# A gated up projection by seven products a pair: every second pair, summed in PSUM

## The chip, the core and the metric

The kernel runs on one core of a Trainium2 chip. The metric is the time of one execution in device microseconds; the smaller the better. Three runs of the kernel before are shown, and one execution of it that was taken by the hardware profiler.

## The reference

One layer of a hybrid encoder trunk in float32: a mixing part (attention and a gated scan, with an output projection), cross attention into 256 memory tokens, and a gated feed-forward part with a convolution over positions. There are 512 positions of width 1024. Only the last part matters here:

```python
def conv_ffn(h, w_up, conv_w, conv_b, w_down):
    n = h.shape[1]
    u = h @ w_up                                  # (512 x 1024) @ (1024 x 5632)
    half = CONV_W // 2
    up = jnp.pad(u, ((0, 0), (half, half), (0, 0)))
    acc = conv_b
    for j in range(CONV_W):                       # CONV_W = 3
        acc = acc + up[:, j:j + n] * conv_w[j]
    gate, val = jnp.split(acc, 2, axis=-1)
    return (jax.nn.silu(gate) * val) @ w_down     # (512 x 2816) @ (2816 x 1024)
```

## The kernel before

**Arithmetic.** Each float32 matrix is split into a rounded high part and a low part (the rest), and each product is made of three matmuls: high by high, high by low, low by high (`mm3`, L296 to L298). The three accumulate in one PSUM bank.

**Weights.** A weight unit is a block of 128 x 1024 float32. SyncE loads it into a raw room (`load_w`, L207); ScalarE casts its high part (L240); the low part is made by DVE (L242), or, for some, by a negation on ScalarE (L247) and an accumulating DMA from DRAM issued by GpSimd (L248). High and low parts lie in four slots, `wh` and `wl`; a unit's cast waits until TensorE is done with the unit that held the slot. Raw rooms are few too: a load waits until the last reader of the room's block is done. Units are asked for up to three ahead, loads up to seven (`issue_ahead`).

**The up projection.** The 5632 columns are 22 pairs of 128 gate columns and 128 value columns. Pairs 0 and 1 come first, then `for i in range(2, NF)` runs pair 2 to 21. A plain pair takes two units, gate and value, each 24 matmuls of 512 columns (positions) into a bank. After each, `conv` makes the convolution: ScalarE scales (L1120), DVE adds the two neighbours (L1121, L1123), for the gate ScalarE takes the silu (L1126), for the value DVE multiplies gate and value (L1134).

**Pairs in seven products.** The pairs in `UP_S` see the 512 positions as two halves (near and far) and the product as one of 2 x 2 blocks, with seven block products in place of eight, in the form of Strassen and Winograd. The factors on the left are sums of h, `s1` to `s4`, made once by `full_h` and `sum_of_h` (DVE L1161, L1165, and the low parts by `split`, L139 and L140). The factors on the right are four units: two blocks from DRAM ("diag" and "side", which hold w11, w22, w12, w21 in some order) and two that DVE makes from them ("sums" with t3 and t1, "last" with t4) in `add_blocks` (L215, L218, L222). Each of the seven products is 12 matmuls of 256 columns. Before, they go to three banks, two regions each, and DVE combines them (L1197 to L1206); only w21 adds onto w11 in PSUM, as the sixth of the seven.

**What sets the order.** The program text gives the order of work, and a scheduler places each engine's instructions by it and by when inputs and rooms come free. On the chip each engine runs its own instructions in the order that it was given; semaphores hold an instruction until its inputs are there and its room is free. `tc.issue_after` puts one instruction behind another in that order.

**Sums for the down projection.** The last stage uses seven products too. Its sums of w_down blocks are built in DRAM: SyncE copies seeds (L266), GpSimd adds onto them by accumulating DMAs (L269), each behind a small copy of its own (L254) at the units in `adds_at`.

The list of products and of sums of h before:

```python
UP_PRODUCTS = (("w11", 0), ("w22", 1), ("t2", 0), ("w21", 1), ("t3", 1), ("t1", 0), ("t4", 0))
of_h = [(s1, a21, a22), (s2, a11, s1), (s3, a21, a11), (s4, a12, s2)]
```

Of the kernel before, what the change touches and what calls it, by code (L numbers as in the profile page):

```python
# [14 lines left out]
ALU = mybir.AluOpType  # L15
# [3 lines left out]
P = 128  # L19
# [6 lines left out]
FF = 2816  # L26
NF = FF // P
EPS = 1e-6
UP_S = (6, 8, 10, 12, 14, 16, 18)
N_MIX, N_WHOLE = 66, 110 - 2 * len(UP_S)  # L30
N_DOWN = N_WHOLE + 4 * len(UP_S)
N_UNITS = N_DOWN + 42
# [2 lines left out]
PRODUCTS = (("w11", "b"), ("t2", "s"), ("t1", "c"), ("w22", "o"), ("t3", "s"), ("t4", "c"), ("w21", "b"))  # L35
SUMS = (("t1", "w11", "w12"), ("t3", "w22", "w12"), ("t2", "w22", "t1"), ("t4", "w21", "t2"))
BLOCKS = ("w11", "w12", "w21", "w22")
UP_PRODUCTS = (("w11", 0), ("w22", 1), ("t2", 0), ("w21", 1), ("t3", 1), ("t1", 0), ("t4", 0))
LAY_AHEAD, LOAD_AHEAD = 3, (7, 5)
SIDES_AT = (19, 20)  # L40
LOW_FROM = {"diag": 0, "side": 512}
SEEDS_AT = frozenset(range(28, 46)) | frozenset(range(60, 66))
ADDS_AT = frozenset(range(56, 62))
NEG_GROUP = frozenset((p, 1) for p in (2, 5, 6))
AHEAD = 3
HOLD_BLOCK = 4
# [61 lines left out]
def layer(tc, io, out):  # L108
    nc = tc.nc
# [8 lines left out]
    t4 = pool("t4", bufs=2)  # L118
    t2 = pool("t2", bufs=4)
# [12 lines left out]
    def tmp2(shape=(P, 512), dt=F32, tag="ta"):  # L132
        return t2.tile(list(shape), dt, name="tmp2", tag=tag, bufs=TMP_BUFS[tag])
# [13 lines left out]
    def half(c):  # L147
        return slice(c * 512, c * 512 + 512)
# [4 lines left out]
    sums, pair_sums = {}, {}  # L153
# [56 lines left out]
    def add_blocks(kind, raw, ahead):  # L210
        if kind == "diag":
            both = vp.tile([P, 1024], F32, name="both", tag="vv")
            mid = ahead[:, :512]
            with tc.issue_after(last_low[0]):
                nc.vector.tensor_tensor(out=both.rearrange("p (a n) -> p a n", a=2),  # L215
                                        in0=raw.rearrange("p (a n) -> p a n", a=2),
                                        in1=mid[:, None, :].to_broadcast([P, 2, 512]), op=ALU.add)
            nc.vector.tensor_add(mid, both[:, :512], raw[:, half(1)])  # L218
            pair_sums["sums"] = both
        elif kind == "side":  # L220
            pair_sums["last"] = tmp2(tag="tq")
            nc.vector.tensor_add(pair_sums["last"], raw[:, :512], raw[:, half(1)])  # L222

    raws = deque()

# [64 lines left out]
    def take():  # L290
        taken[0] += 1
        issue_ahead()
        return pending.popleft()

    def mm3(o, a, b, start, stop, again=False):
        nc.tensor.matmul(o, a[0], b[0], start=start, stop=False, skip_group_check=again)  # L296
        nc.tensor.matmul(o, a[0], b[1], start=False, stop=False, skip_group_check=again)  # L297
        last_mm[0] = nc.tensor.matmul(o, a[1], b[0], start=False, stop=stop, skip_group_check=again).ins  # L298
# [213 lines left out]
    for j in range(4):  # L512
# [8 lines left out]
        for k in range(2):  # L521
            kc = 2 * j + k
# [632 lines left out]
    s1, s2, s3, s4 = wide[0][:, 0], wide[0][:, 1], wide[1][:, 0], wide[1][:, 1]  # L1155
    (a11, a21), (a12, a22) = [[f[:, :, t] for t in half_t] for f in fulls]
    sums_of_h = [(t[:, 0], t[:, 1]) for t in (big([P, 2, 4, 256], F32R) for _ in range(4))]
    of_h = [(s1, a21, a22), (s2, a11, s1), (s3, a21, a11), (s4, a12, s2)]

    def full_h(k):  # L1160
        nc.vector.tensor_add(fulls[k], hT.hi[k].bitcast(F32), hT.lo[k].bitcast(F32))  # L1161
# [13 lines left out]
    def next_bank():  # L1175
        tag_at[0] += 1
        return bank(up_tags[(tag_at[0] - 1) % 4])

    def strassen_pair(i):
        g, m, n = next_bank(), next_bank(), next_bank()  # L1180
        place = {"w11": (g, near), "t2": (m, far), "t1": (m, near), "w22": (n, near), "t3": (n, far),
                 "w21": (g, near), "t4": (g, far)}
        two, more, val = tmp2(tag="th"), tmp2(tag="th"), tmp2(tag="tq")
        for k, (name, at_w) in enumerate(UP_PRODUCTS):
            if k % 2 == 0:
                w = take()
            (hi, lo), cols = left_h[name]
            o, at = place[name]
            o = o[:, at]
            for kc in range(4):  # L1190
                wc = slice(at_w * 512 + kc * P, at_w * 512 + kc * P + P)
                mm3(o, (w[0][:, wc], w[1][:, wc]), (hi[:, kc, cols], lo[:, kc, cols]), kc == 0 and name != "w21",
                    kc == 3, name == "w21")
            if name == "w11":
                nc.scalar.copy(two[:, near], o)
            elif name == "t2":
                nc.vector.tensor_sub(two[:, far], o, two[:, near])  # L1197
            elif name == "t3":
                nc.vector.tensor_add(more[:, far], o, two[:, far])
            elif name == "t1":  # L1200
                nc.vector.tensor_add(more[:, near], o, two[:, far])
                nc.vector.tensor_tensor(out=val.rearrange("p (a t) -> p a t", a=2),
                                        in0=n.rearrange("p (a t) -> p a t", a=2),
                                        in1=more[:, None, near].to_broadcast([P, 2, 256]), op=ALU.add)
            elif name == "t4":
                nc.vector.tensor_sub(o, o, more[:, far])  # L1206
        conv(0, i, g)
        conv(1, i, val)

    for i in range(2, NF):  # L1210
# [131 lines left out]
def pack_up(w_up):  # L1342
    w = w_up.reshape(2, 4, P, 2, NF, P).transpose(4, 0, 3, 2, 1, 5)
    w = w.reshape(NF, 4, P, 512)[list(UP_S)]
    return w[:, [0, 3, 1, 2]].reshape(len(UP_S), 2, 2, P, 512).transpose(0, 1, 3, 2, 4).reshape(len(UP_S), 2, P, 1024)


def pack_down(w_down):
# [49 lines left out]
```

## Time and profile before

| what | value |
|---|---|
| median of three runs | 814.41 us (813.89 to 815.04) |
| the profiled execution | 814.31 us |
| its span, first to last instruction | 812.5 us |
| granted clock of TensorE | 0.998 |
| L296 to L298 of the weights-by-h kind with 512 or 256 columns into one bank, each line | some 120 us, 344 matmuls |
| L240, casts of weight units | 113.8 us in 110 casts, 1036 ns each |
| L242, low parts on DVE | 92.9 us in 77, 1209 ns each |
| weight loads by SyncE | 91 of 512 KB, 3.4 us to landing |
| accumulating loads of low parts by GpSimd | 33 of 512 KB, 6.8 us to landing |

Times are from the span's start. A row of the timeline has a start, a duration, the engine, the line and the operation; in square brackets stands how long the engine stood idle before it and whose end ended that. Matmuls are pipelined, so a matmul's duration is longer than the distance to the next one: 512 columns show 0.39 us and follow each other every 0.227 us, 256 columns 0.28 and 0.12. DVE's and ScalarE's durations overlap a little likewise. PEclk is the share of TensorE's full clock that was granted. In rows of DMAs the last number is the time from issue to landing.

### The profile page before, as it was taken

To read this page: it belongs to the slowest core of one execution; us is meant where nothing else is said; L and a number is where in the kernel's file an instruction comes from. 1 tells how busy PE (TensorE), PEld (TensorE's weight loads), DVE (VectorE), ACT (ScalarE), POOL (GpSimd) and SP (SyncE) were. 2 spreads that over 40 slices of the span, in tenths; PEclk is the share of its full clock that TensorE was granted. 3 is DMA by queue.
4 is the path that set the end of the run, shared out by engine and by line. 5 is a ranking of instruction groups with operands and counts; after the bars stand their busy time and mean duration, and the time that the engine had idled before them with its cause. 6 is when DMAs were issued, how large, how long until landed. Compare 5 with 4: busy or idle time off the path is not lost.

```text
span 812.5 us, 11696 instructions
## 1 busy us (share of the span) xinstructions
PE 800.7 (99%) x4390; PEld 688.4 (85%) x4390; DVE 582.7 (72%) x878; ACT 482.0 (59%) x797; POOL 136.5 (17%) x213
## 2 busy tenths in 40 slices
PE   9999999999999999999999999999999999999996
PEld 7888878899988888888888898899999998888885
DVE  5467576698896765855453767987777788888765
ACT  6675774677978873645443553665555545566651
POOL 0111201334213102301011311211111111000301
PEclk9999999999999999999999999999999999999999
DMA  8596666679777752256634158776765667278842
GB/s 300 198 267 164 137 148 130 146 187 267 206 193 191 186 188 109 86 173 170 167 117 143 33 165 205 161 199 164 187 166 141 160 187 179 91 211 277 241 127 104
DMA packets 42458, 139.61 MB, mean 172 GB/s; under 512 B 5281, under 2 KB 6561, under 8 KB 42401
## 3 DMA queue, kind: packets, MB, share of 16 engines
q1 hardware_dynamic: 28944, 97.43, 35.0%
q0 software_dynamic: 12160, 38.54, 26.8%
q10 hardware_dynamic: 1296, 2.89, 1.0%
q8 instruction: 34, 0.56, 0.3%
q14 instruction: 24, 0.19, 0.1%
HBM read 135.17 MB, written 25.17 MB: 197 GB/s over the span
## 4 chain that ended last, share of the span: by engine, by line
PE 89%; DVE 4%; ACT 4%; issue 1%; DMA 1%; POOL 1%; SPq 0%; DVEq 0%; POOLq 0%
PE ps_b L298 9%; PE ps_b L297 9%; PE ps_b L296 9%; PE ps_s L296 7%; PE ps_s L298 7%; PE ps_s L297 7%; PE ps_o L296 5%; PE ps_o L298 5%; PE ps_o L297 5%; PE ps_c L296 4%; PE ps_c L298 4%; PE ps_c L297 4%; PE ps_c L685 2%; PE ps_o L942 1%; PE ps_o L931 1%; PE ps_s L921 1%
## 5 line engine op out<-in xcount | busy, mean ns | idle before, releaser
L240 ACT CAST wh<-raw 128x1024 fp32r<-128x1024 f32 x110 | 113.8, 1036 | 106.9 <-PE ps_b L297 30.2
L242 DVE TENSOR_TENSOR wl<-raw,wh 128x1024 fp32r<-128x1024 f32 (+1 forms) x77 | 92.9, 1209 | 72.5 <-ACT wh L240 72.4
L296 PE MATMUL ps_b<-big,wh 128*128 128x512 f32 (+1 forms) x344 | 122.2, 355 | 0.0
L298 PE MATMUL ps_b<-big,wl 128*128 128x512 f32 (+1 forms) x344 | 120.9, 351 | 0.0
L297 PE MATMUL ps_b<-big,wh 128*128 128x512 f32 (+1 forms) x344 | 120.4, 350 | 0.0
L298 PEld LDWEIGHTS ps_b<-big,wl 128*128 128x128 f32 x344 | 65.0, 189 | 8.7
L297 PEld LDWEIGHTS ps_b<-big,wh 128*128 128x128 f32 x344 | 65.1, 189 | 8.2
L296 PEld LDWEIGHTS ps_b<-big,wh 128*128 128x128 f32 x344 | 65.1, 189 | 8.0
L711 DVE TENSOR_TENSOR big<-big 128x512 f32<-128x512 f32 x64 | 48.3, 769 | 9.2 <-ACT tmp L682 4.8
L296 PE MATMUL ps_s<-wh,big 128*128 128x512 f32 (+1 forms) x140 | 53.5, 383 | 0.1
L297 PE MATMUL ps_s<-wl,big 128*128 128x512 f32 (+1 forms) x140 | 53.2, 380 | 0.0
L298 PE MATMUL ps_s<-wh,big 128*128 128x512 f32 (+1 forms) x140 | 53.0, 379 | 0.0
L248 POOL DMA_DIRECT2D wl<-in_w_dram x33 | 29.4, 890 | 118.7 <-ACT wl L247 105.6
L140 DVE TENSOR_TENSOR big<-ps_o,big 128x512 fp32r<-128x512 f32 x54 | 36.8, 686 | 11.5 <-ACT big L139 11.3
L139 ACT CAST big<-ps_o 128x512 fp32r<-128x512 f32 x54 | 31.8, 589 | 17.0 <-PE ps_o L1047 7.5
L296 PE MATMUL ps_s<-big,wh 128*128 128x256 f32 (+1 forms) x120 | 40.0, 333 | 0.0
L297 PE MATMUL ps_s<-big,wh 128*128 128x256 f32 (+1 forms) x120 | 39.9, 333 | 0.0
L298 PE MATMUL ps_s<-big,wl 128*128 128x256 f32 (+1 forms) x120 | 39.9, 332 | 0.0
L297 PE MATMUL ps_c<-big,wh 128*128 128x256 f32 (+1 forms) x120 | 39.1, 325 | 0.0
L296 PE MATMUL ps_c<-big,wh 128*128 128x256 f32 (+1 forms) x120 | 39.1, 325 | 0.0
L298 PE MATMUL ps_c<-big,wl 128*128 128x256 f32 (+1 forms) x120 | 39.0, 325 | 0.0
L296 PE MATMUL ps_o<-wh,big 128*128 128x512 f32 (+1 forms) x102 | 38.8, 380 | 0.0
(322 smaller groups left out, 2147.1 us busy)
## 6 DMA issues: line engine op xcount, KB each, us to landing
raw<-in_w_dram SPq DMA_DIRECT2D x91, 512.0 KB, 3.4
wl<-in_w_dram POOLq DMA_DIRECT2D x33, 512.0 KB, 6.8
sum_t<-in_wd_dram SPq DMA_DIRECT2D x20, 512.0 KB, 6.0
tmp<-in_wu_dram SPq DMA_DIRECT2D x14, 512.0 KB, 7.3
sum_t<-in_wd_dram POOLq DMA_DIRECT2D x10, 512.0 KB, 8.1
sum_t<-sum_t POOLq DMA_DIRECT2D x10, 512.0 KB, 7.4
big<-sum_t SPq DMA_DIRECT2D x10, 512.0 KB, 4.9
raw<-sum_t SPq DMA_DIRECT2D x10, 512.0 KB, 3.8
```

What stands on the lines that cost most here:

```text
L139: nc.scalar.copy(hi, src)
L140: (eng or nc.vector).tensor_sub(lo, src, hi.bitcast(F32))
L240: nc.scalar.copy(wh, raw)
L242: last_low[0] = nc.vector.tensor_sub(wl[:, :by_dma], raw[:, :by_dma], wh[:, :by_dma].bitcast(F32)).ins
L248: nc.gpsimd.dma_start(wl[:, by_dma:], source(i)[:, by_dma:], accum_op=ALU.add)
L296: nc.tensor.matmul(o, a[0], b[0], start=start, stop=False, skip_group_check=again)
L297: nc.tensor.matmul(o, a[0], b[1], start=False, stop=False, skip_group_check=again)
L298: last_mm[0] = nc.tensor.matmul(o, a[1], b[0], start=False, stop=stop, skip_group_check=again).ins
L685: nc.tensor.matmul(o[:, b, :], kc[:, blk(b)], qc[:, blk(b)] if m == 1 else pat(qk, b * P, [[2 * m, P // (2 * m)], [T + m, 2], [1, m]]), st ...
L711: nc.vector.tensor_tensor(out=c, in0=c, in1=pat(tt, toff + off, [[2, npair], [gap, 2], [0, m]]), op=ALU.mult)
L921: nc.tensor.matmul(s, qT[h // 4][:, h % 4, blk(qb)], kT[:, 2 * (h // 4) + c, :], start=c == 0, stop=c == 1)
L931: nc.tensor.transpose(o[:, c, :], e[:, 0, blk(c)], ident)
```

## The change

`UP_S` has eight pairs instead of seven, the odd ones from 5 to 19 instead of the even ones from 6 to 18. Inside such a pair the form of the seven products is another one: the order is w11, w21, t2, t3, t1, t4, w22; w11, t3 and t4 accumulate on top of each other in one region of a bank, t2, t1 and w22 in one region of a second, and w21 stands alone in a third. Each quarter of the result is one difference or sum of PSUM and of a copy: ScalarE copies w11 (L1195), t2 (L1199) and t3 (L1201) out of PSUM when each is complete, and DVE makes gate near (L1197, w21 plus w11), value far (L1203, t1 less t3's copy), gate far (L1205, t4 less t2's copy) and value near (L1208, w22 less t2's copy). The gate lies in SBUF now. A copy must be done before the next product accumulates onto its region.

Diag and side hold other blocks (`pack_up`), `add_blocks` makes all sums when diag is asked for, in four operations of 512 columns (L217, L218, L219, L222), and only L217 is put behind the low part before it; `s3` has the other sign. Two of the additions for the down projection move from pair 5 to the units 62 and 63. Lines shift: L139 and L140 become L141 and L142, L207 becomes L209.

```diff
@@ -26,7 +26,7 @@
 FF = 2816
 NF = FF // P
 EPS = 1e-6
-UP_S = (6, 8, 10, 12, 14, 16, 18)
+UP_S = (5, 7, 9, 11, 13, 15, 17, 19)
 N_MIX, N_WHOLE = 66, 110 - 2 * len(UP_S)
 N_DOWN = N_WHOLE + 4 * len(UP_S)
 N_UNITS = N_DOWN + 42
@@ -35,12 +35,14 @@
 PRODUCTS = (("w11", "b"), ("t2", "s"), ("t1", "c"), ("w22", "o"), ("t3", "s"), ("t4", "c"), ("w21", "b"))
 SUMS = (("t1", "w11", "w12"), ("t3", "w22", "w12"), ("t2", "w22", "t1"), ("t4", "w21", "t2"))
 BLOCKS = ("w11", "w12", "w21", "w22")
-UP_PRODUCTS = (("w11", 0), ("w22", 1), ("t2", 0), ("w21", 1), ("t3", 1), ("t1", 0), ("t4", 0))
+UP_PRODUCTS = (("w11", 0), ("w21", 1), ("t2", 0), ("t3", 1), ("t1", 0), ("t4", 0), ("w22", 1))
+UP_TAKES = {"w11": "diag", "t2": "side", "t3": "sums", "t4": "last"}
+UP_FROM = {"w11": "diag", "w21": "diag", "t2": "side", "t3": "sums", "t1": "sums", "t4": "last", "w22": "side"}
 LAY_AHEAD, LOAD_AHEAD = 3, (7, 5)
 SIDES_AT = (19, 20)
 LOW_FROM = {"diag": 0, "side": 512}
 SEEDS_AT = frozenset(range(28, 46)) | frozenset(range(60, 66))
-ADDS_AT = frozenset(range(56, 62))
+ADDS_AT = frozenset(range(56, 64))
 NEG_GROUP = frozenset((p, 1) for p in (2, 5, 6))
 AHEAD = 3
 HOLD_BLOCK = 4
@@ -212,14 +214,12 @@
             both = vp.tile([P, 1024], F32, name="both", tag="vv")
             mid = ahead[:, :512]
             with tc.issue_after(last_low[0]):
-                nc.vector.tensor_tensor(out=both.rearrange("p (a n) -> p a n", a=2),
-                                        in0=raw.rearrange("p (a n) -> p a n", a=2),
-                                        in1=mid[:, None, :].to_broadcast([P, 2, 512]), op=ALU.add)
-            nc.vector.tensor_add(mid, both[:, :512], raw[:, half(1)])
+                nc.vector.tensor_add(both[:, :512], raw[:, :512], mid)
+            nc.vector.tensor_add(both[:, half(1)], ahead[:, half(1)], mid)
+            nc.vector.tensor_add(mid, both[:, :512], ahead[:, half(1)])
             pair_sums["sums"] = both
-        elif kind == "side":
             pair_sums["last"] = tmp2(tag="tq")
-            nc.vector.tensor_add(pair_sums["last"], raw[:, :512], raw[:, half(1)])
+            nc.vector.tensor_add(pair_sums["last"], raw[:, half(1)], mid)
 
     raws = deque()
 
@@ -1155,7 +1155,7 @@
     s1, s2, s3, s4 = wide[0][:, 0], wide[0][:, 1], wide[1][:, 0], wide[1][:, 1]
     (a11, a21), (a12, a22) = [[f[:, :, t] for t in half_t] for f in fulls]
     sums_of_h = [(t[:, 0], t[:, 1]) for t in (big([P, 2, 4, 256], F32R) for _ in range(4))]
-    of_h = [(s1, a21, a22), (s2, a11, s1), (s3, a21, a11), (s4, a12, s2)]
+    of_h = [(s1, a21, a22), (s2, a11, s1), (s3, a11, a21), (s4, a12, s2)]
 
     def full_h(k):
         nc.vector.tensor_add(fulls[k], hT.hi[k].bitcast(F32), hT.lo[k].bitcast(F32))
@@ -1177,34 +1177,35 @@
         return bank(up_tags[(tag_at[0] - 1) % 4])
 
     def strassen_pair(i):
-        g, m, n = next_bank(), next_bank(), next_bank()
-        place = {"w11": (g, near), "t2": (m, far), "t1": (m, near), "w22": (n, near), "t3": (n, far),
-                 "w21": (g, near), "t4": (g, far)}
-        two, more, val = tmp2(tag="th"), tmp2(tag="th"), tmp2(tag="tq")
-        for k, (name, at_w) in enumerate(UP_PRODUCTS):
-            if k % 2 == 0:
-                w = take()
+        a, b, c = next_bank(), next_bank(), next_bank()
+        place = {"w11": a, "t3": a, "t4": a, "t2": b, "t1": b, "w22": b, "w21": c}
+        kept, part = tmp2(tag="th"), tmp2(tag="th")
+        gate, val = tmp2(tag="th"), tmp2(tag="tq")
+        w = {}
+        for name, at_w in UP_PRODUCTS:
+            if name in UP_TAKES:
+                w[UP_TAKES[name]] = take()
+            wh, wl = w[UP_FROM[name]]
             (hi, lo), cols = left_h[name]
-            o, at = place[name]
-            o = o[:, at]
+            o, again = place[name][:, near], name not in ("w11", "t2", "w21")
             for kc in range(4):
                 wc = slice(at_w * 512 + kc * P, at_w * 512 + kc * P + P)
-                mm3(o, (w[0][:, wc], w[1][:, wc]), (hi[:, kc, cols], lo[:, kc, cols]), kc == 0 and name != "w21",
-                    kc == 3, name == "w21")
+                mm3(o, (wh[:, wc], wl[:, wc]), (hi[:, kc, cols], lo[:, kc, cols]), kc == 0 and not again, kc == 3, again)
             if name == "w11":
-                nc.scalar.copy(two[:, near], o)
+                nc.scalar.copy(kept[:, near], o)
+            elif name == "w21":
+                nc.vector.tensor_add(gate[:, near], o, kept[:, near])
             elif name == "t2":
-                nc.vector.tensor_sub(two[:, far], o, two[:, near])
+                nc.scalar.copy(kept[:, far], o)
             elif name == "t3":
-                nc.vector.tensor_add(more[:, far], o, two[:, far])
+                nc.scalar.copy(part[:, near], o)
             elif name == "t1":
-                nc.vector.tensor_add(more[:, near], o, two[:, far])
-                nc.vector.tensor_tensor(out=val.rearrange("p (a t) -> p a t", a=2),
-                                        in0=n.rearrange("p (a t) -> p a t", a=2),
-                                        in1=more[:, None, near].to_broadcast([P, 2, 256]), op=ALU.add)
+                nc.vector.tensor_sub(val[:, far], o, part[:, near])
             elif name == "t4":
-                nc.vector.tensor_sub(o, o, more[:, far])
-        conv(0, i, g)
+                nc.vector.tensor_sub(gate[:, far], o, kept[:, far])
+                conv(0, i, gate)
+            else:
+                nc.vector.tensor_sub(val[:, near], o, kept[:, near])
         conv(1, i, val)
 
     for i in range(2, NF):
@@ -1342,7 +1343,7 @@
 def pack_up(w_up):
     w = w_up.reshape(2, 4, P, 2, NF, P).transpose(4, 0, 3, 2, 1, 5)
     w = w.reshape(NF, 4, P, 512)[list(UP_S)]
-    return w[:, [0, 3, 1, 2]].reshape(len(UP_S), 2, 2, P, 512).transpose(0, 1, 3, 2, 4).reshape(len(UP_S), 2, P, 1024)
+    return w[:, [0, 2, 1, 3]].reshape(len(UP_S), 2, 2, P, 512).transpose(0, 1, 3, 2, 4).reshape(len(UP_S), 2, P, 1024)
 
 
 def pack_down(w_down):

```

Where instructions moved on DVE, in three places. The first is pair 4, while the sums of h are made. Before, DVE had there, behind the L1123 of pair 3's gate (the first row printed is the one after it):

```order
L242 TENSOR_TENSOR wl<-raw,wh 128x1024
L1165 TENSOR_TENSOR big<-big 128x1024 x2
L1121 SCALAR_TENSOR_TENSOR tmp_4928<-ps_o,cw,tmp_4928 128x511
L140 TENSOR_TENSOR big<-big 128x1024
L1123 SCALAR_TENSOR_TENSOR tmp_4928<-ps_o,cw,tmp_4928 128x511
L140 TENSOR_TENSOR big<-big 128x1024
L1134 TENSOR_TENSOR big<-tmp_4886,tmp_4928 128x512
L242 TENSOR_TENSOR wl<-raw,wh 128x1024
L1121 SCALAR_TENSOR_TENSOR tmp_4970<-ps_b,cw,tmp_4970 128x511
L215 TENSOR_TENSOR both<-tmp_4821,tmp_4860 128x1024
L1123 SCALAR_TENSOR_TENSOR tmp_4970<-ps_b,cw,tmp_4970 128x511
```

Now, from the same L1123 on:

```order
L217 TENSOR_TENSOR both<-raw 128x512
L218 TENSOR_TENSOR both<-raw 128x512
L1165 TENSOR_TENSOR big<-big 128x1024
L219 TENSOR_TENSOR raw<-both,raw 128x512
L1121 SCALAR_TENSOR_TENSOR tmp_4935<-ps_o,cw,tmp_4935 128x511
L222 TENSOR_TENSOR tmp_4907<-raw 128x512
L1123 SCALAR_TENSOR_TENSOR tmp_4935<-ps_o,cw,tmp_4935 128x511
L142 TENSOR_TENSOR big<-big 128x1024
L1134 TENSOR_TENSOR big<-tmp_4886,tmp_4935 128x512
L1165 TENSOR_TENSOR big<-big 128x1024
L242 TENSOR_TENSOR wl<-raw,wh 128x512
L1121 SCALAR_TENSOR_TENSOR tmp_4979<-ps_b,cw,tmp_4979 128x511
```

The four operations of `add_blocks` for the first pair in seven products, half a low part and three rows for sums of h stand ahead of pair 4's gate L1121, where before two low parts and four operations on sums of h stood; the first sum of blocks (L215) had come behind it.

The second place follows directly, up to the differences of the first such pair, which is pair 5 now (its w21 is read by L1197, its t1 by L1203):

```order
L142 TENSOR_TENSOR big<-big 128x1024
L1123 SCALAR_TENSOR_TENSOR tmp_4979<-ps_b,cw,tmp_4979 128x511
L242 TENSOR_TENSOR wl<-both,wh 128x1024
L218 TENSOR_TENSOR both<-raw 128x512
L242 TENSOR_TENSOR wl<-tmp_4907,wh 128x512
L1121 SCALAR_TENSOR_TENSOR tmp_5015<-ps_s,cw,tmp_5015 128x511
L1123 SCALAR_TENSOR_TENSOR tmp_5015<-ps_s,cw,tmp_5015 128x511
L1197 TENSOR_TENSOR tmp_5025<-ps_b,tmp_5023 128x256
L1134 TENSOR_TENSOR big<-tmp_4979,tmp_5015 128x512
L242 TENSOR_TENSOR wl<-tmp_4909,wh 128x1024
L1203 TENSOR_TENSOR tmp_5026<-ps_o,tmp_5024 128x256
```

The L218 in it reads the side block of the following such pair, pair 7: it is not held behind a low part as L217 is, and stands ahead of this pair's last low parts, L1197 and L1203.

The third place is a plain pair between two such pairs, later on. Before, from the product of the pair in seven products (L1134) to the plain pair's own:

```order
L1134 TENSOR_TENSOR big<-tmp_5839,tmp_5844 128x512
L242 TENSOR_TENSOR wl<-both,wh 128x1024
L1121 SCALAR_TENSOR_TENSOR tmp_5884<-ps_c,cw,tmp_5884 128x511
L1123 SCALAR_TENSOR_TENSOR tmp_5884<-ps_c,cw,tmp_5884 128x511
L242 TENSOR_TENSOR wl<-tmp_5856,wh 128x512
L1121 SCALAR_TENSOR_TENSOR tmp_5920<-ps_o,cw,tmp_5920 128x511
L1123 SCALAR_TENSOR_TENSOR tmp_5920<-ps_o,cw,tmp_5920 128x511
L1134 TENSOR_TENSOR big<-tmp_5884,tmp_5920 128x512
L242 TENSOR_TENSOR wl<-raw,wh 128x1024
```

Now:

```order
L1134 TENSOR_TENSOR big<-tmp_5769,tmp_5787 128x512
L242 TENSOR_TENSOR wl<-both,wh 128x1024
L1121 SCALAR_TENSOR_TENSOR tmp_5825<-ps_b,cw,tmp_5825 128x511
L218 TENSOR_TENSOR both<-raw 128x512
L1123 SCALAR_TENSOR_TENSOR tmp_5825<-ps_b,cw,tmp_5825 128x511
L242 TENSOR_TENSOR wl<-tmp_5752,wh 128x512
L1121 SCALAR_TENSOR_TENSOR tmp_5861<-ps_s,cw,tmp_5861 128x511
L1123 SCALAR_TENSOR_TENSOR tmp_5861<-ps_s,cw,tmp_5861 128x511
L1134 TENSOR_TENSOR big<-tmp_5825,tmp_5861 128x512
```

An L218 now stands between L1121 and L1123 of the plain pair's gate; it reads the side block of the pair in seven products after the next. Before, all sums of blocks stood behind the next pair's first products.

## The prediction

> **What bounds the kernel now.** I read the page from its first two parts to the chain, then cut the span into stages.
>
> ```profile
> span 812.5 us, 11696 instructions
> PE 800.7 (99%) x4390; PEld 688.4 (85%) x4390; DVE 582.7 (72%) x878; ACT 482.0 (59%) x797; POOL 136.5 (17%) x213
> PE 89%; DVE 4%; ACT 4%; issue 1%; DMA 1%; POOL 1%; SPq 0%; DVEq 0%; POOLq 0%
> ```
>
> TensorE is busy almost throughout and carries 89% of the chain. The span is 812.5 us; the profiled execution took 814.31 us, so 1.8 us lie around the span. The median shown, 814.41 us, differs from that execution by 0.1 us; I take the sum against 814.31.
>
> The second view is busy time by stage: pairs 0 to 5, then the stretch in which pairs in seven products and plain pairs alternate.
>
> ```profile
> core 0: us, PE busy (x) PEld busy (x) DVE busy (x) ACT busy (x) POOL busy (x), PEclk, DMA share, GB/s
> 478.00:531.00 53.00, 53.00 (x276) 45.64 (x275) 44.15 (x49) 28.08 (x34) 11.77 (x18) 1.00 0.73 170
> 531.00:663.00 132.00, 132.00 (x841) 120.48 (x840) 102.80 (x146) 73.39 (x95) 17.63 (x26) 1.00 0.66 165
> ```
>
> In both stages TensorE has no gap at full clock, while DVE is busy 83% (44.15 of 53.00) and 78%. So TensorE's own work sets the time, and DVE, in order, has little room: an instruction that stands waiting there holds up much behind it.
>
> **The change part by part.** First TensorE's work. These rows of the timeline (start, duration) are the first matmuls of the two units of pair 4, of the first two products of pair 6, and of pair 8:
>
> ```profile
> 509.95 0.39 PE L296 MATMUL ps_b<-big,wh 128*128 128x512 f32 x1
> 515.39 0.39 PE L296 MATMUL ps_s<-big,wh 128*128 128x512 f32 x1
> 531.71 0.28 PE L296 MATMUL ps_b<-big,wh 128*128 128x256 f32 x1
> 533.14 0.28 PE L296 MATMUL ps_c<-big,wh 128*128 128x256 f32 x1
> 552.75 0.28 PE L296 MATMUL ps_s<-big,wh 128*128 128x256 f32 x1
> ```
>
> A unit of 24 matmuls of 512 columns takes 515.39 − 509.95 = 5.44 us, so a plain pair 10.88. A product of 12 matmuls of 256 columns takes 533.14 − 531.71 = 1.43, near 1.44 over a whole pair, so seven take 10.08. One pair more in seven products gives **−0.80 us**. The rest of the change moves no matmul elsewhere.
>
> Second, the first such pair. It is now pair 5: it starts where pair 4 ends, 515.39 + 5.44 = 520.83, not at 531.71. In between, DVE builds the sums of h (L1165 and L142, which was L140). Its rows there before:
>
> ```profile
> 513.63 0.75 DVE L1123 SCALAR_TENSOR_TENSOR tmp<-ps_c,cw,tmp 128x511 f32<-128x511 f32 x1
> 514.29 1.22 DVE L242 TENSOR_TENSOR wl<-raw,wh 128x1024 fp32r<-128x1024 f32 x1
> 515.42 2.35 DVE L1165 TENSOR_TENSOR big<-big 128x1024 f32<-128x1024 f32 x2
> 517.69 0.74 DVE L1121 SCALAR_TENSOR_TENSOR tmp<-ps_o,cw,tmp 128x511 f32<-128x511 f32 x1
> 518.35 1.22 DVE L140 TENSOR_TENSOR big<-big 128x1024 fp32r<-128x1024 f32 x1
> 521.28 0.69 DVE L1134 TENSOR_TENSOR big<-tmp,tmp 128x512 f32<-128x512 f32 x1
> 521.88 1.22 DVE L242 TENSOR_TENSOR wl<-raw,wh 128x1024 fp32r<-128x1024 f32 x1
> 560.80 0.42 DVE L1199 TENSOR_TENSOR tmp<-ps_o,tmp 128x256 f32<-128x256 f32 x1
> 561.14 1.21 DVE L215 TENSOR_TENSOR both<-tmp,tmp 128x1024 f32<-128x1024 f32 x1
> ```
>
> DVE's instructions here follow each other with no idle time, so I take start to start: 1024 columns 1.13 us, 511 columns 0.66, 512 columns 0.60 (521.28 to 521.88), 256 columns 0.34 (560.80 to 561.14). Up to the L1123 at 513.63 the order is unchanged. After it, by the order shown ahead, come six of 512 (L217, L218, L219, L222, L1134, L242), four of 1024 (L1165 and L142, twice each) and three of 511 before pair 4's own gate L1123: 3.60 + 4.52 + 1.98 = 10.10. That L1123 starts at 514.29 + 10.10 = 524.39 and ends at 525.14.
>
> Who waits for it: ScalarE, whose order from there is the one that it had before.
>
> ```profile
> 532.39 0.63 ACT L1126 ACTIVATE tmp<-tmp 128x512 f32<-128x512 f32 x1 [2.18 <-DVE tmp L1123]
> 532.93 0.60 ACT L240 CAST wh<-tmp 128x512 fp32r<-128x512 f32 x1
> 533.44 0.78 ACT L1120 ACTIVATE tmp<-ps_o,cw 128x512 f32<-128x512 f32 x1
> 534.11 0.36 ACT L1195 COPY tmp<-ps_b 128x256 f32<-128x256 f32 x1
> ```
>
> The silu waits for L1123; behind it stand a cast, the other half's L1120, and the copy of w11 (L1195), which ends 534.47 − 532.39 = 2.08 after the silu's start. In the change that is 525.17 + 2.08 = 527.25. Before, this lateness cost nothing, because w11's bank was not written again until the seventh product. Now t3, the fourth, accumulates onto it. Without waits t3 would start at 520.83 + 3 × 1.44 = 525.15, so TensorE waits **2.1 us**. Behind t3 on TensorE's queue stands all that is left of the kernel.
>
> Then w22, the seventh product, accumulates onto the bank that L1203 (t1's difference) reads, and on DVE L1203 stands behind an L218 of the next such pair, which needs a block that SP can load only when this pair's side room is free, after its L242. That L242 is the tenth of the list after 514.29; it ends at 522.69. How long such a load takes:
>
> ```profile
> raw<-in_w_dram SPq DMA_DIRECT2D x1, 512.0 KB, 5.2
> tmp<-in_wu_dram SPq DMA_DIRECT2D x1, 512.0 KB, 9.1
> tmp<-in_wu_dram SPq DMA_DIRECT2D x1, 512.0 KB, 8.3
> tmp<-in_wu_dram SPq DMA_DIRECT2D x1, 512.0 KB, 8.8
> tmp<-in_wu_dram SPq DMA_DIRECT2D x1, 512.0 KB, 7.5
> tmp<-in_wu_dram SPq DMA_DIRECT2D x1, 512.0 KB, 8.4
> raw<-in_w_dram SPq DMA_DIRECT2D x91, 512.0 KB, 3.4
> ```
>
> The last number is us from issue to landing: the load issued at 523.17, those of side blocks issued at 544.46, 565.45, 586.42, 607.40 and 628.38, and the median over the kernel. Here I take the nearest in time, 5.2: 522.75 + 5.2 = 527.95. From L218's start to L1203's end DVE needs 0.60 + 0.60 + 0.66 + 0.66 + 0.34 + 0.60 + 1.13 + 0.42 = 5.0, so 533.0. With the first wait in it w22 would start at 527.25 + 3 × 1.44 = 531.57: **1.4 us** more. By a load of 3.4 it is nothing, by one of 6.9 (midway to those of the later pairs) 3.1. So the first pair costs 3.5, between 2.1 and 5.2.
>
> Third, the seven later pairs. There the same L218 stands between L1121 and L1123 of the plain pair's gate half, so ScalarE's silu, and behind it the copy of w11, wait for a load. When is that load issued? Count from the pair's first matmul, T0 (552.75 above).
>
> ```profile
> 561.46 1.05 ACT L240 CAST wh<-tmp 128x1024 fp32r<-128x1024 f32 x1 [1.83 <-PE ps_c L297]
> 562.59 1.06 ACT L247 ACTIVATE wl<-wh 128x1024 fp32r<-128x1024 f32 x1
> 564.74 0.68 DVE L242 TENSOR_TENSOR wl<-tmp,wh 128x512 fp32r<-128x512 f32 x1
> ```
>
> Before, the side half's L242 ends at 565.42 and the load goes at T0 + 12.7. Now ScalarE's L247 ends as before (T0 + 10.9, since the sixth product frees the same slot), then come L1120 (0.67) and the side's cast (1.05): T0 + 12.6; L242 follows, and the load goes at T0 + 13.45. The next such pair starts at T0 + 20.96 (10.08 + 10.88), its t3 at T0 + 25.28. Back from there: silu to copy 2.08, L1123 0.75, L218 0.60, with the hand-overs some 3.5, so the load must land by T0 + 21.7, **8.24 us** after issue. The five rows above go over that by 0.86, 0.06, 0.56, 0 and 0.16: a mean of 0.33. But the diag block's load, ahead in the same queue, also goes later: its room is free only after L222, which stands behind the sums' low part, L217, L1205, L219 and L1208, about 1.5 us later than before, so the side's load lands later by up to 1.5 and is issued only 0.7 later. With 0.8 on each of the five: 1.66, 0.86, 1.36, 0.06 and 0.96, a mean of 0.98. Six loads count (the first pair's own is costed above). The ends are 0 and 6 × 0.98 = 5.9; I take the rows as they stand, 0.33 × 6 = **+2.0**.
>
> Costed at nothing: the two further copies on ScalarE (0.36 each, 59% busy; t1 and t4 wait for them and have some 0.7 us), DVE's narrower operations (four of 512 in place of one of 1024 and two of 512, but fewer of 256, behind the waits named), and the two additions moved from pair 5 to the units before (POOL is 17% busy; the seeds were loaded long before). If their cover goes, each costs at most its own duration a pair, 0.3 to 0.7.
>
> Sum: 814.31 − 0.80 + 3.5 + 2.0 = **819.0 us**.
>
> [...] The clock before:
>
> ```profile
> 470.00:474.00 4.00, 3.84 (x33) 3.63 (x32) 3.79 (x6) 1.12 (x3) 0.00 (x0) 1.00 0.51 152
> ```
>
> Here TensorE idled 0.16 us within these 4 us and the granted clock stayed 1.00. [...]
>
> **The rivals.** *The waits run into each other* (0.15): W1's low part on DVE stands behind the late L218, so the slots come free later, the next loads go later, and each of the six loads costs 1.2 rather than 0.33 (between the 0.86 and the 1.66 of the longest row): 817.0 + 7.2 = 824.2. For it speaks the 9.1; against it that a waiting TensorE also leaves the loads more time.
>
> *Only the first pair waits* (0.18): all later loads land within 8.24 us; 817.0. The 7.5 speaks for it, the other four rows against.
>
> *Not slower: the first pair's loads are quick and the later ones in time* (0.22). The place is L218 ahead of L1203. If its load lands within 3.8 us of issue, like the median of 3.4, the second wait is gone and only t3's 2.1 stays: 814.31 − 0.80 + 2.1 = 815.6. If also pair 4's gate L1123 came 2 us earlier than I count, TensorE would have no gap: 813.5. Against it: DVE had no idle time to give there.
>
> *The clock falls* (0.03): the first pair's waits are one long gap and the product behind it runs at twice its 1.43: 819.0 + 1.4 = 820.4.
>
> The change doing something else than it says is no rival: the order holds eight pairs of 84 matmuls.
>
> **How the numbers follow.** The forecast holds 0.42. What a measurement of this kernel tells from no change is about 0.2%, here 812.8 to 816.0. Same is the third rival, less some for its faster end: 0.20. Faster needs more than the 0.80 of TensorE's work: 0.04. Slower 0.76. The range leaves out the gapless end below and joined waits above: 814.2 to 825.
>
> **What would show it.** Right: in the profile after, a gap on TensorE before t3 of pair 5 near 525, ended by ScalarE's L1195, and one before w22, ended by DVE's L1203; in later pairs short gaps before t3, each after an L218 that waited for a DMA. Wrong: no gap at either place, L218's load landing within 3.8 us, or gaps at slots of weights instead (L240, L242, the accumulate L248).

## The result and the profile after

The changed kernel takes **834.53 us** (median of four runs, 833.1 to 835.94); the kernel before took 814.6 us beside it. The ratio is 1.0241, with a 95% interval of 1.0227 to 1.0256. The forecast was 819.0 us with a range up to 825: the direction was right, the size was not. The profiled execution took 834.96 us.

The page after, the lines that answer to those of before: span, engines, the chain by engine and by line.

```profile
span 833.2 us, 11802 instructions
PE 807.7 (97%) x4426; PEld 694.7 (83%) x4426; DVE 583.5 (70%) x887; ACT 489.2 (59%) x818; POOL 138.2 (17%) x215
...
PE 20%; DMA 8%; DVE 7%; ACT 2%; issue 2%; POOL 0%; DVEq 0%; POOLq 0%; ACTq 0%
DMA raw<-in_wu_dram 7%; PE ps_c L296 2%; PE ps_c L297 2%; PE ps_c L298 2%; DVE wl L242 2%; PE ps_s L298 2%; PE ps_s L296 2%; PE ps_s L297 2%; PE ps_b L297 1%; PE ps_b L296 1%; PE ps_o L296 1%; PE ps_b L298 1%; PE ps_o L297 1%; PE ps_o L298 1%; DMA wl<-in_wu_dram 1%
```

The chain no longer runs on TensorE alone: 7% of the span is a load into a raw room from `in_wu_dram`, the blocks of the pairs in seven products. And TensorE is busy 7.0 us longer than before (807.7 against 800.7) although it has 0.8 us less to do. Both need an explanation.

The first is in TensorE's own waits. These are all the rows of its timeline from pair 5 to pair 19 that have a wait (in brackets: how long it stood idle, and whose end released it).

```profile
526.51 0.38 PE L296 MATMUL ps_c<-big,wh 128*128 128x256 f32 x1 [1.01 <-ACT tmp L1195]
531.57 0.38 PE L296 MATMUL ps_o<-big,wh 128*128 128x256 f32 x1 [0.50 <-DVE tmp L1203]
545.41 0.38 PE L298 MATMUL ps_o<-big,wl 128*128 128x256 f32 x1 [1.00 <-DMA wl<-in_wu_dram]
551.84 0.39 PE L296 MATMUL ps_o<-big,wh 128*128 128x256 f32 x1 [2.10 <-ACT tmp L1195]
575.45 0.38 PE L296 MATMUL ps_b<-big,wh 128*128 128x256 f32 x1 [0.88 <-ACT tmp L1195]
599.20 0.39 PE L296 MATMUL ps_s<-big,wh 128*128 128x256 f32 x1 [2.14 <-ACT tmp L1195]
622.91 0.38 PE L296 MATMUL ps_c<-big,wh 128*128 128x256 f32 x1 [1.00 <-ACT tmp L1195]
647.24 0.39 PE L296 MATMUL ps_o<-big,wh 128*128 128x256 f32 x1 [3.10 <-ACT tmp L1195]
671.62 0.39 PE L296 MATMUL ps_b<-big,wh 128*128 128x256 f32 x1 [1.66 <-ACT tmp L1195]
689.11 0.39 PE L298 MATMUL ps_s<-big,wl 128*128 128x256 f32 x1 [0.33 <-DMA wl<-in_wu_dram]
```

Seven of the eight pairs wait before t3 for the copy of w11, 11.9 us in all; the other waits add 1.8. Pair 19, the last, has no such wait, and no L218 stands ahead of it.

What delays the copy is seen on DVE and ScalarE around pair 9, whose t3 is the 575.45 above:

```profile
566.91 0.75 DVE L1121 SCALAR_TENSOR_TENSOR tmp<-ps_c,cw,tmp 128x511 f32<-128x511 f32 x1
571.87 0.69 DVE L218 TENSOR_TENSOR both<-raw 128x512 f32<-128x512 f32 x1 [4.21 <-DMA raw<-in_wu_dram]
572.48 0.74 DVE L1123 SCALAR_TENSOR_TENSOR tmp<-ps_c,cw,tmp 128x511 f32<-128x511 f32 x1
573.32 0.63 ACT L1126 ACTIVATE tmp<-tmp 128x512 f32<-128x512 f32 x1 [6.96 <-DVE tmp L1123]
573.85 0.60 ACT L240 CAST wh<-tmp 128x512 fp32r<-128x512 f32 x1
574.36 0.77 ACT L1120 ACTIVATE tmp<-ps_o,cw 128x512 f32<-128x512 f32 x1
575.04 0.36 ACT L1195 COPY tmp<-ps_b 128x256 f32<-128x256 f32 x1
```

Read it downwards. DVE finishes L1121 and stands 4.21 us before L218, until its load has landed. L1123 is next in DVE's order, though it needs no load; ScalarE's silu needs L1123 and has stood 6.96 us; the cast, the other half's L1120 and the copy of w11 stand behind the silu. The copy ends at 575.40, t3 starts at 575.45. From the landing to t3 it is 3.6 us. Over the stage DVE stood 33.5 us before L218, in seven waits:

```profile
DVE both L218 <- DMA raw<-in_wu_dram: 33.5, 7, 6.7
```

The second thing is the clock. Windows of 5 us, two for each of the three longest waits; the third number from the end is the granted clock (before, it was 1.00 in these stages):

```profile
550.00:555.00 5.00, 3.16 (x15) 3.16 (x16) 4.05 (x6) 3.38 (x7) 0.00 (x0) 0.71 0.00 0
555.00:560.00 5.00, 5.00 (x39) 4.87 (x38) 3.24 (x6) 3.19 (x4) 1.02 (x2) 0.95 0.69 157
595.00:600.00 5.00, 2.86 (x24) 2.65 (x23) 3.08 (x5) 2.92 (x6) 0.00 (x0) 0.99 0.12 47
600.00:605.00 5.00, 5.00 (x32) 5.00 (x32) 3.22 (x6) 1.79 (x4) 1.05 (x2) 0.67 0.23 75
645.00:650.00 5.00, 2.76 (x14) 2.76 (x15) 3.67 (x7) 3.41 (x7) 0.00 (x0) 0.77 0.00 0
650.00:655.00 5.00, 5.00 (x38) 4.96 (x37) 3.24 (x6) 3.00 (x4) 1.01 (x2) 0.89 0.57 136
```

A clock of 0.71 over 5 us and 0.95 over the next 5 is 0.29 × 5 + 0.05 × 5 = 1.7 us of full clock not granted. The same sum around 600 (0.99 and 0.67) and around 647 (0.77 and 0.89) gives 1.7 each. What it costs is read from the matmuls themselves: 17, 16 and 16 of them stand 0.213 us apart in place of 0.12 (from 551.84 to 555.45, from 599.90 to 603.31, from 647.72 to 651.12), which is 1.5 to 1.6 us more each time, 4.5 us in all. That is the larger part of TensorE's longer busy time.

The account: −0.8 for the pair, 11.9 for L1195, 1.8 for the other waits, 4.5 for the clock make 17.4 of the 20.7 us by which the span grew. Most of the rest lies at the edges of the ten waits. From start to start each is some 0.15 us longer than the idle time shown, 1.6 in all (in pair 7 t2 began at 548.15 us and lasts 1.44, so t3, at 551.84, was 2.25 us late where 2.10 is shown). And at nine of them the matmul after the wait is followed 0.1 us later than usual, 0.9 in all. Some 0.8 us stay open.

### The profile page after: what moved, and what is told of

It reads as the page before. It is cut to its first block, busy times and chain, and to the rows that moved or that the text cites. A ratio compares the mean times of both kernels' runs of the same rounds, so it can differ in the third digit from the quotient of the medians.

```text
span 833.2 us, 11802 instructions
## 1 busy us (share of the span) xinstructions
PE 807.7 (97%) x4426; PEld 694.7 (83%) x4426; DVE 583.5 (70%) x887; ACT 489.2 (59%) x818; POOL 138.2 (17%) x215
## 5 line engine op out<-in xcount | busy, mean ns | idle before, releaser
L242 DVE TENSOR_TENSOR wl<-raw,wh 128x1024 fp32r<-128x1024 f32 (+1 forms) x69 | 78.2, 1135 | 58.1 <-ACT wh L240 58.0
L1126 ACT ACTIVATE tmp<-tmp 128x512 f32<-128x512 f32 x22 | 13.9, 631 | 65.7 <-DVE tmp L1123 65.7
L296 PE MATMUL ps_o<-big,wh 128*128 128x256 f32 (+1 forms) x120 | 40.2, 335 | 5.7 <-ACT tmp L1195 5.2
L142 DVE TENSOR_TENSOR big<-ps_o,big 128x512 fp32r<-128x512 f32 x54 | 36.8, 687 | 11.6 <-ACT big L141 11.3
L254 POOL COPY mark<-wl 128x1 f32<-128x1 f32 x24 | 5.6, 235 | 233.8 <-DVE wl L242 233.8
L141 ACT CAST big<-ps_o 128x512 fp32r<-128x512 f32 x54 | 31.7, 588 | 17.0 <-PE ps_o L1047 7.5
L296 PE MATMUL ps_c<-big,wh 128*128 128x256 f32 (+1 forms) x120 | 39.6, 330 | 2.0 <-ACT tmp L1195 2.0
L296 PE MATMUL ps_s<-big,wh 128*128 128x256 f32 (+1 forms) x120 | 39.5, 329 | 2.1 <-ACT tmp L1195 2.1
L298 PE MATMUL ps_o<-big,wl 128*128 128x256 f32 (+1 forms) x120 | 40.1, 334 | 1.0 <-DMA wl<-in_wu_dram 1.0
```

The lines of the kernel that those rows point to most:

```text
L141: nc.scalar.copy(hi, src)
L142: (eng or nc.vector).tensor_sub(lo, src, hi.bitcast(F32))
L242: last_low[0] = nc.vector.tensor_sub(wl[:, :by_dma], raw[:, :by_dma], wh[:, :by_dma].bitcast(F32)).ins
L254: with tc.issue_after(nc.gpsimd.tensor_copy(mark, wl[:, 0:1].bitcast(F32)).ins):
L1126: last_act[0] = nc.scalar.activation(a, a, ACT.Silu).ins
```

## Experiments

**1. L218 back in its place.** Only the place of one instruction on DVE: the high half of the block sums is put behind the same low part as the low half.

```diff
             with tc.issue_after(last_low[0]):
                 nc.vector.tensor_add(both[:, :512], raw[:, :512], mid)
-            nc.vector.tensor_add(both[:, half(1)], ahead[:, half(1)], mid)
+                nc.vector.tensor_add(both[:, half(1)], ahead[:, half(1)], mid)
```

> The changed kernel with L218 (the high half of a pair's block sums) put behind the same low part as L217, so that it stands inside the next pair's products again and no longer ahead of L1123. Theory 1 (the in-order chain L218, L1123, silu, copy of w11 waits for a late load): the waits for L1195 of 0.9 to 3.1 us go in all pairs but the first, where some 1.0 us stays because L1123 is late for another reason; the clock stays at 1.00; 814.3 - 0.8 + 1.2 = about 814.7 us. Theory 2 (the loads are late by themselves and everything that needs them is): the gaps move to the weights, accumulating loads or low parts, and 820 us or more remain. Theory 3 (accumulating t3 on w11 so soon after is too tight by itself): the gaps before t3 stay, about 830 us.

Measured: 817.02 us against 814.84 us of the kernel before beside it, ratio 1.0024 (1.0014 to 1.0034). All waits of TensorE in the up projection are gone but one, in the first pair, and a window of lower clock comes with that one:

```profile
527.86 0.58 PE L296 MATMUL ps_c<-big,wh 128*128 128x256 f32 x1 [2.32 <-ACT tmp L1195]
```

```profile
520.00:540.00 20.00, 17.68 (x112) 16.44 (x111) 17.90 (x26) 12.70 (x18) 3.18 (x5) 0.91 0.57 143
```

So the place of L218 alone costs 834.5 − 817.0 = 17.5 us. Theory 1 holds for the later pairs; theories 2 and 3 fall. The 2.3 us that are left are the expectation's miss: with the clock (1 − 0.91 = 0.09 over 20 us, 1.8 us) the first pair still costs 4.1 in the profiled execution.

**2. The old form with the same eight pairs.** `UP_S` and `ADDS_AT` of the change in the kernel before, nothing else.

```diff
-UP_S = (6, 8, 10, 12, 14, 16, 18)
+UP_S = (5, 7, 9, 11, 13, 15, 17, 19)
-ADDS_AT = frozenset(range(56, 62))
+ADDS_AT = frozenset(range(56, 64))
```

> The kernel before with the eight pairs 5 to 19 and the two moved additions, and its old products, banks and differences. Theory 1: nothing waits for L1195, the first pair may lose up to 1 us to the sums of h; 813.5 to 814.7 us. Rival (a pair in seven products at 5 or an eighth pair is what costs): a good part of the 20 us shows, 818 us or more.

Measured: 817.18 us, ratio 1.0027 (1.0014 to 1.0041), between what theory 1 and the rival gave: 2.3 us over before, far from the 20. Two waits, both in the first pair, both for sums of h:

```profile
524.25 0.38 PE L296 MATMUL ps_b<-big,wh 128*128 128x256 f32 x1 [1.09 <-ACT big L139]
526.11 0.39 PE L297 MATMUL ps_b<-big,wh 128*128 128x256 f32 x1 [1.48 <-DVE big L140]
```

The clock fell behind them too (0.91 from 520 to 540 us). So pair 5 is too early for either form: it costs more than the 0.8 us that the eighth pair saves.

**3. The new form with the old seven pairs.** The changed kernel with `UP_S` and `ADDS_AT` of before.

> The changed kernel with the seven pairs 6 to 18 and the additions of before: the new form alone. Theory 1: waits before t3 by L1195 in five of the seven pairs, 1 to 3 us each, and a clock below 1 after the longest: of the 20.9 us that the eight pairs lose, all but the first pair's 2.0 and the last one's, so 828 to 833 us. Rival (the eighth pair and its place cost it): 814 to 816 us.

Measured: 833.23 us, ratio 1.0203 (1.017 to 1.0235), 0.2 us above what theory 1 gave; the four executions lie between 828.27 and 833.38. Six waits for L1195, 12.7 us in all, the longest 4.22; the clock at 0.91 and 0.92 in two windows of 20 us. The new form with L218 where the scheduler put it costs this with seven pairs as with eight.

**4. The new form, L218 behind the low part, eight pairs from 6 to 20.**

```diff
-UP_S = (5, 7, 9, 11, 13, 15, 17, 19)
+UP_S = (6, 8, 10, 12, 14, 16, 18, 20)
```

> The new form with L218 behind the low part, and eight pairs at 6, 8 to 20 in place of 5 to 19: the first one comes 10.9 us later, when the sums of h are done. Theory 1: no gap on TensorE in the up projection at all, the clock stays at 1.00, 814.3 - 0.8 = 813.5 us, a little faster than before. Rival (the first pair in seven products waits wherever it is): a gap of 1 to 2.5 us before its t3 and a lower clock behind it, 816 to 818 us as with the pairs from 5 on.

Measured: 815.08 us against 814.78, ratio 1.001 (0.9996 to 1.0025). TensorE waits for nothing in the up projection and the clock is 1.00 there, as theory 1 has it. So the first pair waits when it comes at 5, where the sums of h are not yet done, and not at 6. The 0.8 us are not to be seen in the time: the interval takes in both no change and a loss of 0.2%, and hardly a gain. In its profile the span is 813.0 us, 0.5 over that of before. The gain is there in the stage itself: from the first matmul of pair 6 to the first of the down stage it takes 700.39 − 532.36 = 168.03 us, before 700.38 − 531.71 = 168.67. But pair 6 starts 0.65 us later in this execution, behind slightly longer waits in the first 60 us, and the down stage takes 0.5 us more.

**5. L218 left where it was, the copy of w11 ahead of the silu.** Now the other end of the chain: the silu and the product of gate and value of a plain pair are issued behind the copy of w11 of the pair that follows.

```diff
+        if i + 1 in UP_S and i > 1:
+            late.append(lambda: join(c, i, a))
+        else:
+            join(c, i, a)
...
-                nc.scalar.copy(kept[:, near], o)
+                copied = nc.scalar.copy(kept[:, near], o).ins
+                with tc.issue_after(copied):
+                    while late:
+                        late.pop(0)()
```

`join` holds the silu, or the product, as `conv` had it.

> The changed kernel with L218 left where the change put it, waiting for the late load; only ScalarE's order is changed: the silu of the plain pair ahead of a pair in seven products, and the product of gate and value, come behind the copy of w11. Theory 1 (what stops TensorE is the chain L218, L1123, silu, copy of w11 in two in-order engines): DVE still waits for the load before L218, but the gaps by L1195 go, also in the first pair; 813.5 to 815 us. Theory 2 (the late loads are the cause, by whatever road): gaps come back at low parts, slots or L1203, 820 us or more.

Measured: 825.72 us, ratio 1.0128 (1.0115 to 1.0142). Both theories had a part. No wait for the copy of w11 is left, and no wait is longer than 1.5 us, so the clock stays at 1.00. But 11 us over before remain, in small waits at other places. From the view of what TensorE waited for (us in total, times, the longest; L1210 is the copy of t2 here):

```profile
PE ps_o L298 <- DMA wl<-in_wu_dram: 2.0, 2, 1.4
PE ps_b L298 <- DMA wl<-in_wu_dram: 1.6, 2, 1.0
PE ps_s L298 <- DMA wl<-in_wu_dram: 1.3, 2, 0.9
PE ps_s L296 <- ACT tmp L1210: 0.8, 2, 0.4
...
```

The largest are for accumulating loads of low parts. So the loads stay late as long as L218 stands where it is, whether or not the copy of w11 waits for it. The view of DMA issues from 540 to 680 us shows it: loads of the pairs' blocks, median time to landing, in the kernel before, after, in experiment 1 and in this one, one row each:

```profile
tmp<-in_wu_dram SPq DMA_DIRECT2D x10, 512.0 KB, 7.6
```

```profile
raw<-in_wu_dram SPq DMA_DIRECT2D x10, 512.0 KB, 9.5
```

```profile
raw<-in_wu_dram SPq DMA_DIRECT2D x10, 512.0 KB, 7.3
```

```profile
raw<-in_wu_dram SPq DMA_DIRECT2D x10, 512.0 KB, 10.2
```

Why they take longer shows on SyncE. Four loads are issued for each pair in seven products and its plain neighbour: two plain units, diag, side (each row is two loads; start of the first, and time from there to the end of the second). After, then experiment 1:

```profile
578.92 2.23 SPq L209 DMA_DIRECT2D tmp<-in_w_dram  x2
583.33 1.56 SPq L209 DMA_DIRECT2D raw<-in_wu_dram  x2
```

```profile
572.37 4.65 SPq L209 DMA_DIRECT2D tmp<-in_w_dram  x2
579.80 1.55 SPq L209 DMA_DIRECT2D raw<-in_wu_dram  x2
```

After, the four are issued within 583.33 + 1.56 − 578.92 = 6.0 us here, in experiment 1 within 9.0. The first plain unit's room is free only when its low part on DVE (L242) is done, and that stands behind L218 and L1123. So the instruction that waits for a load also holds back the next loads, which then go closer together and take longer. The closer they go, the longer the side block's load takes: in the profile after the four go within some 6 us (5.5 to 6.0) and within 7.5 us by turns, and that load takes 11.0 to 11.8 us in the first case and 9.3 to 10.1 in the second. No run moved the plain units' loads alone, so that the closeness itself makes them longer is what the rows suggest, not shown by an edit of its own. TensorE's waits are not what does it: in experiment 5 they are small, the four go within 5.7 us, and the loads are the slowest.

**6. Both repairs**, with the pairs 5 to 19.

> Both repairs: L218 behind the low part, and the copy of w11 ahead of the silu, pairs 5 to 19. Theory 1: no gap, also not in the first pair, and a clock of 1.00: 813.5 us. Rival: the first pair still waits, by DVE's sums of h, for something else: 815 to 818 us.

Measured: 816.51 us, ratio 1.0018 (1.0008 to 1.0028); single runs lie between 814.65 and 818.55. The profiled execution, one of the quicker ones (815.5 us), has two waits and a clock of 1.00: 0.32 us in the first pair for the difference on t1, and 1.02 us in pair 7 for an accumulating load that took 11.7 us. The four loads of SyncE go within 6.1 us ahead of that one, as they do after; that this too comes of the first pair's lateness is likely, not shown. The rival is right: pair 5 still waits for something else.

**7 and 8. A probe of the clock that did not probe it.** On the kernel of experiment 4 ScalarE's copy of w11 was made 6 to 18 times, to give waits of known length.

> A probe of the clock on the kernel with eight pairs from 6 on, which has no gap: ScalarE's copy of w11 is made 6, 8, 9, 11, 12, 14, 16 and 18 times in the eight pairs, so that TensorE waits some 0.3 to 4 us before t3, longer from pair to pair. The runs so far had the granted clock fall behind gaps of 2.0 to 4.2 us and not behind 1.7. If that is a matter of the gap's length alone, the clock falls behind each gap over 2 us and costs about 1.7 us each time; if only gaps over 3.4 us lower it, behind the last one or two; if the phase of a free running window decides, behind some of those over 2 us.

> The same probe with the counts in falling order, 18 to 6: the same gaps in other places, so that place and length are told apart.

Measured: 821.49 and 828.28 us, one run each. The scheduler knew of the copies and let other products pass t3 on TensorE, so the waits meant did not come about; the longest was 1.75 us, for an accumulating load, and the clock stayed at 1.00 behind it.

**9. The old form with an eighth pair at 20**, `ADDS_AT` as in the change.

> The kernel before with an eighth pair at 20 and the two moved additions: pairs 6, 8 to 20 in the old form. It removes 0.8 us of TensorE's work and moves the first pair nowhere: 814.8 (this chip's time of before) - 0.8 = 814.0 us if nothing waits. Rival (the last pair in seven products so near to the down stage costs what it saves): no difference from before.

Measured: 816.85 us, ratio 1.0023 (1.0014 to 1.0032). The rival is nearer, but the eighth pair costs more than it saves. In the up projection one wait of 0.63 us is left; the down stage begins with one of 1.36 us for its left factors (L140), which DVE makes later now that pair 20 has more work for it.

**10. The probe again, with TensorE's order held.** As 7, with each matmul group of the pairs put behind the one before it, and 14, 9, 20, 11, 17, 7, 24 and 12 copies.

```diff
+                for _ in range((14, 9, 20, 11, 17, 7, 24, 12)[UP_S.index(i)]):
+                    copied = nc.scalar.copy(kept[:, near], o).ins
...
+                with tc.issue_after(last_mm[0]):
+                    mm3(o, (wh[:, wc], wl[:, wc]), (hi[:, kc, cols], lo[:, kc, cols]), kc == 0 and not again, kc == 3, again)
```

> The probe of the clock again, with TensorE's matmuls of the pairs held in the program's order, so that t3 can't be passed by others: the kernel with eight pairs from 6 on and L218 behind the low part, and ScalarE's copy of w11 made 14, 9, 20, 11, 17, 7, 24 and 12 times, for gaps before t3 of some 0.5 to 5 us. If the length of a gap alone decides, all gaps over some 2 us lower the granted clock and cost 1.7 us more each; if a free running window decides, gaps of 2 to 3.4 us do it in some pairs and not in others; if only gaps over 3.4 us count, those of 14 copies and fewer leave it at 1.00.

Measured: 860.57 us, one run. The waits before t3 were 4.18, 1.78, 6.24, 2.59, 5.03, 0.98, 7.85 and 3.00 us. Windows of 4 us around the second, the sixth and the last:

```profile
564.00:568.00 4.00, 3.42 (x17) 3.42 (x18) 0.42 (x1) 0.87 (x3) 0.90 (x2) 0.60 0.78 183
672.00:676.00 4.00, 3.72 (x31) 3.72 (x32) 1.11 (x3) 1.26 (x3) 1.02 (x2) 1.00 0.52 151
728.00:732.00 4.00, 4.00 (x24) 4.00 (x23) 1.45 (x4) 1.22 (x2) 0.00 (x0) 0.58 0.82 148
```

Behind every wait but that of 0.98 us the clock fell, to 0.58 to 0.65 over 4 us behind those up to 4.2. Pair 8, with the wait of 1.78, took 13.6 us (558.3 to 571.9) where a pair without waits takes 10.08: 1.78 for the wait, 1.6 for 17 matmuls that stand 0.213 us apart in place of 0.12, the rest at the edges of the wait.

## Why the prediction was wrong

**TensorE's work, −0.80.** Right as far as the runs can tell: without waits a pair takes 10.07 us in the new form too (from 553.34 to 563.41 in experiment 4), and the stage there is 0.64 us shorter. That the time of the whole kernel does not show it is below what these runs resolve.

**The mechanism** was right in each link that it named: the first pair's late L1123, the copy of w11 behind the silu, L218 ahead of L1123 and of L1203, the load behind it. The rows above are the ones that the prediction asked for, with the waits by L1195 before t3, by L1203 before w22, and an L218 that waited for a DMA. Two further waits, 1.00 and 0.33 us for accumulating loads of low parts, are of the kind that it had named as a sign of being wrong. Experiment 1 shows that L218's place is the cause of all but the first pair.

**The first pair, 3.5 us.** Too high: measured 1.01 for t3 and 0.50 for w22, 1.5 us, below even its low end of 2.1. The thirteen operations on DVE took the 10.1 us that were counted (L217 at 513.41, L1123 at 523.53), but they began 0.9 us earlier than in the row of before, and the load landed in 4.4 us where 5.2 was taken. In experiment 1, with the same order of DVE up to there, L217 began at 514.76 and t3's wait was 2.32, against 2.1 forecast. So the start of this chain moves by more than a microsecond from one execution to another.

**The later pairs, +2.0: the step that failed.** The formula held. The load must land within 8.24 us of issue; the loads that block t3 of pairs 9 to 17 took these times:

```profile
raw<-in_wu_dram SPq DMA_DIRECT2D x1, 512.0 KB, 9.3
raw<-in_wu_dram SPq DMA_DIRECT2D x1, 512.0 KB, 11.0
raw<-in_wu_dram SPq DMA_DIRECT2D x1, 512.0 KB, 9.4
raw<-in_wu_dram SPq DMA_DIRECT2D x1, 512.0 KB, 11.5
raw<-in_wu_dram SPq DMA_DIRECT2D x1, 512.0 KB, 10.1
```

Less 8.24 that is 1.1, 2.8, 1.2, 3.3 and 1.9; the waits shown for pairs 9 to 17 are 0.88, 2.14, 1.00, 3.10 and 1.66. The load for pair 7 took 11.8, 3.6 over; TensorE had waited 1.00 shortly before, at 545.41, and then 2.10 at t3. What was wrong is the times put in: those of before, 7.5 to 9.1, a mean excess of 0.33, and at most 0.98 with the two loads going closer together. The prediction counted the diag load's delay, but left the plain units' loads where they were. They too stand behind L218 by way of L242, and all four loads went within 5.5 to 7.5 us, where they had 7.7 before and 9.0 in experiment 1.

**The rival that the waits run into each other** (0.15) named that very road, W1's low part behind the late L218, and was the right one. Its price, 1.2 a load, was too low: the six waits before t3 of pairs 7 to 17 add up to 10.9 us, 1.8 each, where the forecast had 2.0 in all.

**The clock** (0.03, 1.4 us) was about a third of the error. It was priced as one event, at one product of twice its time, behind the first pair's waits joined into one. No run shows that 1.4 us as such. Here waits of 2.1, 2.14 and 3.1 us in later pairs lowered the clock, three times in one execution, 1.5 us each and 4.5 together. The Trainium skill ("TensorE: Matmul & The Clock Gate", section "HAM oscillation — how this bites in real kernels") has the rule that idle gaps over about 3.4 us lower the clock; in its example each fall slows TensorE for 1.67 us and costs half of that. This case differs in both: shorter waits did it, and the slow stretches lasted 3.4 to 3.6 us and cost 1.5. The measurement decides.

**Costed at nothing** and rightly so: the further copies on ScalarE, the narrower sums on DVE, the two moved additions. In experiment 4, which has all of them, nothing waits.

## What to carry to other kernels

An instruction that needs a fresh load and is free to move can be placed by a scheduler well ahead of the load's landing, as L218 was here; in an in-order engine everything behind it then waits for the DMA, so pin it behind something that is known to come later. When a wait is found, ask which loads stand behind it too: load times read from the undisturbed trace no longer hold once their issues bunch. And an idle stretch of TensorE of some 2 us or more may cost 1.5 us beyond its length, so price it with both.

## What the runs showed of the hardware

A wait of TensorE far shorter than 3.4 us can lower the granted clock. With the waits of all runs here in the up projection: none up to 1.75 us alone did; 1.78, 2.02, 2.10 (with 1.00 some 4 us ahead), 2.14, 2.32, 2.59 and all longer ones did; 2.05 and 2.08 in experiment 3 did not, and the pair of 1.09 and 1.48 in experiment 2, with 0.4 us of work between them, did. So near 2 us the length alone does not decide. The Trainium skill ("TensorE: Matmul & The Clock Gate", section "What's actually happening") describes a window of about 3.4 us that runs freely, whatever the kernel does. Behind waits up to 4.22 us the traces have eleven slow stretches, of 2.6 to 3.6 us; five of them last 3.38 to 3.41 (16 matmuls 0.213 us apart, in the profile after and in experiments 2, 3 and 10) and agree with that length. That the phase of such a window decides which waits near 2 us count would fit too, but no run here shows it. The loss per fall, counted on the matmuls behind the wait, was 1.1 to 1.6 us for waits from 1.78 to 4.22 us.
